# Three buffers for gathered keys, a gather one step ahead, and a denser decode, in a hybrid decoder step on one core

## The chip, the core and the metric

The kernel runs on one core of a Trainium2 chip. The metric is the time of one execution on the device in microseconds; lower is better. TensorE (PE) multiplies, VectorE (DVE) and ScalarE (ACT) work element by element, GpSimd (POOL) issues the gathers, and SyncE (SP) issues the plain loads.

## What is computed

One layer of a decoder, for a prompt of 512 tokens and for 8 decode rows that each look back on 4096 cached tokens. Each token goes through a norm, one wide projection, two mixers (softmax attention with a forget bias, "fox", and gated linear attention, "gla"), two sigmoid gates, an output projection `w_o`, and an MLP with squared ReLU. What the change touches is the attention of the 8 decode rows over their paged cache, and the reuse of the MLP's weights for these rows:

```python
def _fox_sample(q, k_new, v_new, logf_new, k_past, v_past, logf_past):
    ...
    lp = (jnp.einsum('bqhd,bkhd->bhqk', q, k_past).astype(F32) * scale
          + jnp.swapaxes(suffix, 1, 2)[:, :, None, :] + cn[..., None])
    ...
    num = (jnp.einsum('bhqk,bkhd->bqhd', pp, v_past.astype(F32))
           + jnp.einsum('bhqk,bkhd->bqhd', pn, v_new.astype(F32)))

def _finish(x, o_fox, o_gla, gfox, ggla, w_fox_out, w_gla_out, w_o, ...):
    u = (jax.nn.sigmoid(gfox) * (o_fox.astype(dt) @ w_fox_out)
         + jax.nn.sigmoid(ggla) * (o_gla.astype(dt) @ w_gla_out))
    x = x + _rmsnorm(u @ w_o, g_post_mix)
    h = _rmsnorm(x, g_pre_mlp)
    m = jnp.square(jax.nn.relu(h @ w_up)) @ w_down
    return x + _rmsnorm(m, g_post_mlp)
```

Keys and values of the cache are 64 MB each, in pages of 128 tokens that a table lists.

## The kernel before

The main line runs the prompt through its stages: projections (`fox_q`, `fox_k`, `fox_v`, `gla_qk`, `gla_vo`), the gate blocks (`gate_f`, `gate_g`, `mix`), `w_o` with its norms (`post`, `wo_each`, `wo_fin`), and four chunks of the MLP, `up(c)` and `down(c)`. Dense products run as three matmuls each on a weight that is split in a high and a low part (L221 on ScalarE, L222 on VectorE). `post` ends with a tail: the last 256 columns are computed block by block of 128 rows, and `wo_fin` then makes the norm of that block (L1182, L216, the power L217 on GpSimd, the sum L1184, eight transposes, L326 and a split).

The decode is a generator of 144 steps, `decode()`: 9 rounds of 16. Step (b, g) scores two of a row's 32 slices of keys for row b (gathered tile `kk` of 0.5 MB, multiply L573 and reduction L574 on VectorE) and, on every second step, multiplies a 1 MB tile of values (`kv`) for row b-1 on TensorE into `pdv`. The last step of a round ends a row: bias, maximum, exponentials (L603 to L619). A gather is issued by `page_load` (L208) on GpSimd's queue; `LK` and `LV` say how many steps ahead, and `BU` how many buffers a tag has. The main line calls `pump(rate)` at every yield: it adds the matmul columns issued since the last call (in units of 2400) times `rate / TAU` to a debt and advances the decode one step per whole unit of debt:

```python
        owed[0] += (clock[0] - seen[0]) * rate / TAU
        while owed[0] >= 1 and (scored[0] or count[0] < NG):
            owed[0] -= 1
```

`PA` to `PE_`, `PF` and `PG` are the rates of the stages. The gate blocks and mixes run at `PC`, the main part of `w_o` at `PD`, its tail at `PF`, the first yields of the MLP at `PG`, the rest at `PE_`. The scheduler below this code places instructions of each engine in an order of its own, in which program order is the priority; every engine then works through its own list in that order.

When the decode is over, `sample_mix` (queued as a side task, one step per yield) takes the 8 rows through gates, `w_fox_out`, `w_o` and the norms and sets `mixed`. From then on `up` carries the 8 rows as extra columns of its own matmuls (`dense_fm2`). Weights that went by earlier are listed in `late` and loaded a second time by `sample_mlp` (tag `kv`, two loads of 0.5 MB for each weight, `sproj_ps` from the unsplit weight). `down(c)` uses its own tile for the 8 rows only where `whole[c]` says that no `up` weight of the chunk was late.

Of the kernel before, what the change touches and what calls it, by code (L numbers as in the profile page):

```python
# [19 lines left out]
NB = 8  # L20
# [3 lines left out]
EPS = 1e-6  # L24
TS = T + NB
FP, LP, LQ = 3, 1, 1
PA, PB, PC, PD, PE_ = 1, 1.2, 0.6, 0.6, 1
LK, LV = 0, 2
TO = 1
PF, PG, HN = 0.8, 1.5, 2  # L30
BU = dict(h=4, c8=9, wh=6, wl=5, raw=5, kk=2, kv=2, td=2, ts=5, qb=2, tj=1, ev=1)
PK = 2
TAU = 3.1
MS = 1
# [1 line left out]
NG, NV = 32 // KJ, 32 // VJ  # L36
# [13 lines left out]
def _emit(ctx, tc, I, O):  # L50
# [591 lines left out]
    def pump(rate):  # L642

        owed[0] += (clock[0] - seen[0]) * rate / TAU
        while owed[0] >= 1 and (scored[0] or count[0] < NG):
            owed[0] -= 1
            count[0] += 1
            if next(dec, "end") == "end":
                over[0] = True
        seen[0] = clock[0]  # L650
# [393 lines left out]
    side = []  # L1044
# [226 lines left out]
            V.tensor_tensor(out=d, in0=p[:, 0:256], in1=d, op=ALU.add)  # L1271
        first[n] = False

    late, whole, mixed = [], [True] * 4, [False]

    def sample_mlp():

# [9 lines left out]
    def up(c, ah, al):  # L1287
# [7 lines left out]
        for n in range(4):  # L1295
            w = take()[0]
            with_sample = mixed[0] and not (c == 0 and n < HN)
            if not with_sample:
                whole[c] = False
                late.append((wup, c, n))  # L1300
            if c == 0 and n < HN:
                for r in (slice(0, 256), slice(256, 512)):
# [19 lines left out]
    def down(c):  # L1322
        def take_(n):
            w, _, raws = take()
            if not whole[c]:
                late.append((wdn, c, n))
            else:
                sample_acc(n, sproj_ps(aS[:, c * 8:c * 8 + 8, :], raws, "x"))
            if c == 3 and n == 3:
                sample_end()  # L1330
            return w
# [25 lines left out]
    def sample_end():  # L1357
        while not over[0]:
            owed[0] += 1
            pump(0)  # L1360
        start_mix()
        drain("mix", "mlp")
        y, x = new_["y"], new_["x"]
        for n in range(2):
            p = ps("x")
            mm(p[0:8, :], sel[:, 0:8], new_["acc"][n], True, True)
            S.copy(out=y[n][0:8, :], in_=p[0:8, :])
        sample_post(y, "g_post_mlp", x)
        for i in range(2):
            nc.sync.dma_start(out=O["y_sample"].rearrange("b l d -> (b l) d")[:, i * 512:(i + 1) * 512], in_=x[i][0:8, :])  # L1370

    def dense_mlp(gen, n, first=()):
        for i, _ in enumerate(gen):
            pump(first[i] if i < len(first) else n)
            if over[0]:
                start_mix()
            beside(MS)

    started = [False]

    def start_mix():
        if not started[0]:
# [40 lines left out]
```

## Time and profile before

| what | value |
|---|---|
| median of three runs | 1068.72 us (1062.19 to 1077.32) |
| the profiled execution | 1074.91 us, span 1073.2 us |
| busy: PE, DVE, ACT, POOL | 93%, 64%, 40%, 25% of the span |
| mean granted clock of TensorE | 0.964 |
| gathers | 128 of keys, 64 of values, 8 of log-forgets |

A busy share is an average over stages; the rows below give it by stage. An instruction's line is that of the helper that records it (L84 for all matmuls), so the tile names tell which product it is: `pmm` the dense products, `pdv` the decode's values, `px` the small products beside.

The stages in the profiled execution, by the first instruction of each on ScalarE or VectorE: projections to 283 us, `gate_f` to 408, `gate_g` and `mix` to 521, `w_o` to 608 (its main part ends about 565), `up(0)` and `down(0)` to 721, and the other three chunks to the end.

### The profile page before, as it was taken

To read this page: it belongs to the slowest core of one execution; us is meant where nothing else is said; L and a number is where in the kernel's file an instruction comes from. 1 tells how busy PE (TensorE), PEld (TensorE's weight loads), DVE (VectorE), ACT (ScalarE), POOL (GpSimd) and SP (SyncE) were. 2 spreads that over 40 slices of the span, in tenths; PEclk is the share of its full clock that TensorE was granted. 3 is DMA by queue.
4 is the path that set the end of the run, shared out by engine and by line. 5 is a ranking of instruction groups with operands and counts; after the bars stand their busy time and mean duration, and the time that the engine had idled before them with its cause. 6 is when DMAs were issued, how large, how long until landed. Compare 5 with 4: busy or idle time off the path is not lost.

```text
span 1073.2 us, 20743 instructions
## 1 busy us (share of the span) xinstructions
PE 995.3 (93%) x8183; PEld 828.5 (77%) x8183; DVE 689.9 (64%) x1238; ACT 426.8 (40%) x1110; POOL 272.8 (25%) x256
## 2 busy tenths in 40 slices
PE   6988899999999899999894799999999799999996
PEld 5987777877967788787683677787787588888995
DVE  8568766876988858887769769667233333233356
ACT  6424444444743423333233443325423453115442
POOL 5132333244332324423434332430100000000001
PEclk9998999999999979999997899999999899999998
DMA  6736788688478637966995687894667366677222
GB/s 199 240 129 209 228 298 289 207 298 309 141 280 311 190 114 254 324 200 209 340 335 178 218 306 260 318 348 138 217 228 239 123 205 213 211 236 233 82 75 86
DMA packets 134279, 242.03 MB, mean 226 GB/s; under 512 B 11627, under 2 KB 105150, under 8 KB 125990
## 3 DMA queue, kind: packets, MB, share of 16 engines
q0 software_dynamic: 28032, 135.28, 35.7%
q1 hardware_dynamic: 106150, 105.43, 31.0%
q8 instruction: 64, 1.05, 0.4%
q14 instruction: 33, 0.27, 0.1%
HBM read 235.14 MB, written 5.47 MB: 224 GB/s over the span
## 4 chain that ended last, share of the span: by engine, by line
PE 64%; DMA 19%; issue 7%; DVE 6%; POOL 1%; ACT 1%; SPq 0%; DVEq 0%; POOLq 0%; ACTq 0%
PE pmm L84 47%; DMA kk<-in_cache_k,ixki 12%; PE px L84 10%; PE pdv L84 5%; DMA kv<-in_cache_v,ixvi 2%; DVE kk L573 2%; DMA kv<-in_w_up 1%; DVE sc L574 1%; DMA kv<-in_w_down 1%; PE pd L84 1%; DMA c<-in_state_gla 1%; DVE wl L222 1%; PE px L684 1%; POOL kk L208 0%; ACT tj L344 0%
## 5 line engine op out<-in xcount | busy, mean ns | idle before, releaser
L84 PE MATMUL pmm<-h,wh 128*128 128x256 f32 (+2 forms) x1696 | 358.7, 307 | 9.9 <-ACT h L221 4.1
L84 PEld LDWEIGHTS pmm<-h,wh 128*128 128x128 f32 x1696 | 276.7, 193 | 47.0 <-issue 19.5
L84 PE MATMUL pmm<-h,wl 128*128 128x256 f32 (+2 forms) x848 | 257.3, 306 | 0.8 <-DVE wl L222 0.8
L208 POOL DMA_INDIRECT kk<-in_cache_k,ixki x128 | 166.2, 1298 | 342.1 <-DVE sc L574 214.2
L84 PE MATMUL pmm<-wh,c 128*128 128x256 f32 x1280 | 233.1, 283 | 6.4 <-DVE c L1039 4.5
L84 PEld LDWEIGHTS pmm<-wh,c 128*128 128x128 f32 x1280 | 196.7, 189 | 28.2 <-issue 16.7
L573 DVE TENSOR_TENSOR kk<-kk,qb 128x1024 f32<-128x1024 f32 x128 | 156.5, 1223 | 92.6 <-DMA kk<-in_cache_k,ixki 90.3
L222 DVE TENSOR_TENSOR wl<-raw,wh 128x512 fp32r<-128x512 f32 x240 | 162.0, 687 | 79.4 <-PE pmm L84 55.8
L221 ACT CAST wh<-raw 128x512 fp32r<-128x512 f32 x240 | 146.4, 619 | 160.9 <-PE pmm L84 99.0
L84 PE MATMUL pmm<-wl,c 128*128 128x256 f32 x640 | 178.8, 282 | 1.6 <-DVE wl L222 1.6
L84 PEld LDWEIGHTS pmm<-h,wl 128*128 128x128 f32 x848 | 162.8, 193 | 12.6 <-issue 4.6
L574 DVE TENSOR_REDUCE sc<-kk 128x16 f32<-128x1024 f32 x128 | 154.9, 1212 | 0.7
L84 PEld LDWEIGHTS pmm<-wl,c 128*128 128x128 f32 x640 | 120.6, 189 | 10.4 <-issue 7.9
L208 POOL DMA_INDIRECT kv<-in_cache_v,ixvi x64 | 69.5, 1086 | 141.1 <-PE pdv L84 115.6
L217 POOL TENSOR_TENSOR rs<-rs,mhalf 128x1 f32<-128x1 f32 (+2 forms) x21 | 16.3, 778 | 292.7 <-DVE rs L216 291.1
L84 PE MATMUL pmm<-wh,h 128*128 128x256 f32 x384 | 77.0, 291 | 0.0
L84 PE MATMUL pdv<-kv,pt 128*32 128x512 f32 x512 | 67.8, 610 | 5.4 <-DMA kv<-in_cache_v,ixvi 5.4
L84 PEld LDWEIGHTS pmm<-wh,h 128*128 128x128 f32 x384 | 60.9, 191 | 5.0 <-issue 4.9
L84 PE MATMUL pmm<-wl,h 128*128 128x256 f32 x192 | 56.5, 295 | 1.0 <-DVE wl L222 1.0
L1338 DVE TENSOR_TENSOR c<-pmm,c 128x256 f32<-128x256 f32 x48 | 18.7, 421 | 57.1 <-PE pmm L84 56.7
L1292 DVE TENSOR_TENSOR c<-td,c 128x256 fp32r<-128x256 f32 (+1 forms) x50 | 24.8, 497 | 32.5 <-ACT td L1291 32.2
L84 PE MATMUL pmm<-c,wh 128*128 128x512 f32 x128 | 42.6, 416 | 1.6 <-DVE c L910 1.3
(335 smaller groups left out, 1099.5 us busy)
## 6 DMA issues: line engine op xcount, KB each, us to landing
raw<-in_w_in SPq DMA_DIRECT2D x80, 256.0 KB
raw<-in_w_up SPq DMA_DIRECT2D x64, 256.0 KB
raw<-in_w_down SPq DMA_DIRECT2D x64, 256.0 KB
kv<-in_w_down SPq DMA_DIRECT2D x24, 512.0 KB
kv<-in_w_up SPq DMA_DIRECT2D x18, 512.0 KB
raw<-in_w_o SPq DMA_DIRECT2D x16, 256.0 KB
kv<-in_w_o SPq DMA_DIRECT2D x8, 512.0 KB
c<-in_x_prompt SPq DMA_DIRECT2D x4, 512.0 KB
```

Source lines behind the costliest of these rows:

```text
L84: PE.matmul(out=out, lhsT=lhsT, rhs=rhs, start=start, stop=stop)
L208: G.indirect_dma_start(out=t, out_offset=None, in_=view, in_offset=bass.IndirectOffsetOnAxis(ap=ix[:, b, g:g + 1], axis=0))
L217: G.tensor_tensor(out=r, in0=a, in1=mhalf[:P, :n], op=ALU.pow)
L221: S.copy(out=hi, in_=raw)
L222: V.tensor_tensor(out=lo, in0=raw, in1=hi.bitcast(F32), op=ALU.subtract)
L573: V.tensor_tensor(out=K3, in0=K3, in1=qb[:, None, :].to_broadcast([128, KJ, 512]), op=ALU.mult)
L574: V.tensor_reduce(out=sc[:, g * 8 * KJ:(g + 1) * 8 * KJ], in_=K.rearrange("p (x d) -> p x d", d=64), axis=AX.X, op=ALU.add)
L684: PE.transpose(out=sp[:, kb * 128:(kb + 1) * 128], in_=P[:, kb * 128:(kb + 1) * 128], identity=ident)
L1292: V.tensor_tensor(out=l, in0=r[:, 0:n], in1=d.bitcast(F32), op=ALU.subtract)
L1338: V.tensor_tensor(out=d, in0=p, in1=d, op=ALU.add)
```

## The change

The rates `PC` and `PD` go from 0.6 to 0.9. Keys have three buffers (`kk=3`), and their gather is issued one step ahead (`LK=1`); `LV` stays 2. For the last round, which has only values, a step costs half a unit of debt. The flags `whole` are gone: `down` uses its own tile for the 8 rows where no `up` weight of its chunk is still in `late`, and `catch_up` queues `sample_mlp` again whenever something is late and no side task is left.

```diff
-PA, PB, PC, PD, PE_ = 1, 1.2, 0.6, 0.6, 1
-LK, LV = 0, 2
+PA, PB, PC, PD, PE_ = 1, 1.2, 0.9, 0.9, 1
+LK, LV = 1, 2
...
-BU = dict(h=4, c8=9, wh=6, wl=5, raw=5, kk=2, kv=2, td=2, ts=5, qb=2, tj=1, ev=1)
+BU = dict(h=4, c8=9, wh=6, wl=5, raw=5, kk=3, kv=2, td=2, ts=5, qb=2, tj=1, ev=1)
...
-        while owed[0] >= 1 and (scored[0] or count[0] < NG):
-            owed[0] -= 1
+        while owed[0] >= (1 if count[0] < NB * NG else 0.5) and (scored[0] or count[0] < NG):
+
+            owed[0] -= 1 if count[0] < NB * NG else 0.5
...
-    late, whole, mixed = [], [True] * 4, [False]
+    late, mixed = [], [False]
...
             if not with_sample:
-                whole[c] = False
                 late.append((wup, c, n))
...
-            if not whole[c]:
+            if not mixed[0] or any(v is wup and e == c for v, e, _ in late):
                 late.append((wdn, c, n))
...
         start_mix()
-        drain("mix", "mlp")
+        drain("mix")
+        catch_up()
+        drain("mlp")
...
                 start_mix()
+            catch_up()
             beside(MS)
 
     started = [False]
+
+    def catch_up():
+        if mixed[0] and late and not side:
+            side.append(("mlp", sample_mlp()))
```

## Rows read from the trace of the kernel before

**Rows 1.** Busy time by stage: PE, weight loads, DVE, ACT, POOL, clock, DMA share, GB/s.

```profile
core 0: us, PE busy (x) PEld busy (x) DVE busy (x) ACT busy (x) POOL busy (x), PEclk, DMA share, GB/s
29.00:135.00 106.00, 94.55 (x746) 86.24 (x745) 73.25 (x126) 41.79 (x114) 29.48 (x22) 0.95 0.63 201
135.00:283.00 148.00, 147.30 (x1120) 113.68 (x1119) 108.85 (x166) 68.81 (x198) 56.73 (x50) 1.00 0.76 269
283.00:408.00 125.00, 117.89 (x1476) 99.25 (x1475) 103.72 (x204) 50.05 (x132) 40.42 (x32) 0.92 0.62 209
408.00:521.00 113.00, 105.70 (x746) 86.57 (x745) 91.87 (x156) 41.56 (x130) 42.77 (x35) 0.97 0.77 266
521.00:571.00 50.00, 49.35 (x401) 43.36 (x401) 34.06 (x54) 17.07 (x47) 17.34 (x17) 0.97 0.87 303
571.00:608.00 37.00, 16.32 (x99) 12.64 (x103) 34.76 (x58) 12.81 (x36) 17.65 (x14) 0.75 0.57 177
608.00:735.00 127.00, 123.76 (x836) 101.28 (x829) 91.09 (x117) 49.72 (x114) 42.68 (x39) 0.98 0.84 297
735.00:1073.00 338.00, 319.85 (x2634) 269.91 (x2632) 128.48 (x284) 126.46 (x308) 10.02 (x13) 0.98 0.54 175
```

**Rows 2.** Waits of PE over the span: us in total, times, longest.

```profile
PE px L323 <- DVE c L1184: 7.0, 1, 7.0
...
PE pdv L84 <- DMA kv<-in_cache_v,ixvi: 5.4, 3, 4.5
...
PE pmm L84 <- DVE c L1039: 4.5, 2, 4.3
...
PE pdv L609 <- DVE mx L606: 3.5, 1, 3.5
PE px L684 <- ACT ts L697: 3.3, 1, 3.3
```

**Rows 3.** The key multiplies (L573) alone by stage: us, DVE busy and their number.

```profile
29.00:283.00 254.00, 61.09 (x50) 0.98 0.71 241
283.00:408.00 125.00, 22.00 (x19) 0.92 0.62 209
408.00:521.00 113.00, 24.43 (x20) 0.97 0.77 266
521.00:571.00 50.00, 8.53 (x7) 0.97 0.87 303
571.00:608.00 37.00, 9.78 (x8) 0.75 0.57 177
608.00:735.00 127.00, 30.64 (x25) 0.98 0.84 297
```

**Rows 4.** L573: min/median/max ns, first and last start; then what DVE waited for.

```profile
L573 DVE TENSOR_TENSOR kk<-kk,qb x128: 1201/1224/1300, 39.5 to 733.7; 128x1024 f32<-128x1024 f32 x128
...
  DMA kk<-in_cache_k,ixki: 90.3, 55
```

**Rows 5.** DVE in order of time: the residual sum of two blocks of the tail.

```profile
565.34 1.28 DVE L1184 SCALAR_TENSOR_TENSOR c<-c,rs,c 128x1024 f32<-128x1024 f32 x1 [0.76 <-POOL rs L217]
...
576.40 1.28 DVE L1184 SCALAR_TENSOR_TENSOR c<-c,rs,c 128x1024 f32<-128x1024 f32 x1
```

**Rows 6.** PE in order of time: half of a second load's product, and its wait.

```profile
902.76 0.64 PE L84 MATMUL px<-kv,c 128*32 128x256 f32 x8 [0.39 <-DMA kv<-in_w_down]
```

**Rows 7.** ACT in order of time: ends of `up` blocks, undivided (740, 745) and halved.

```profile
740.02 0.59 ACT L1289 ACTIVATE td<-pmm 128x512 f32<-128x512 f32 x1
745.41 0.60 ACT L1289 ACTIVATE td<-pmm 128x512 f32<-128x512 f32 x1 [3.47 <-PE pmm L84]
...
1000.97 0.38 ACT L1289 ACTIVATE td<-pmm 128x256 f32<-128x256 f32 x1
...
1012.09 0.38 ACT L1289 ACTIVATE td<-pmm 128x256 f32<-128x256 f32 x1 [0.23 <-PE pmm L84]
```

**Rows 8.** GpSimd's gathers of keys, and busy time in a stretch with a full DVE.

```profile
L208 POOL DMA_INDIRECT kk<-in_cache_k,ixki x128: 932/1020/4222, 24.1 to 728.9; - x128
...
493.00:498.00 5.00, 5.00 (x29) 3.86 (x29) 4.71 (x8) 1.22 (x4) 4.40 (x2) 1.00 0.53 141
```

## The prediction

> **What bounds the kernel now.** I read the busy time of every engine by stage first, because the share over the whole span hides where an engine waits. TensorE (PE) is the bound: from 135 to 283 us it works 147.3 of 148 us, and from 735 to the end 319.9 of 338 [rows 1]. So a step of the decode is worth something only where PE stands still. That is in three places: 29 to 135 us (11.4 us idle), 283 to 521 us (7.1 and 7.3 us), and above all 571 to 608 us, where PE works 16.3 of 37 us while VectorE (DVE) works 34.8 of 37 and the granted clock is 0.75 [rows 1]. That last stretch is the tail of the w_o stage, four row blocks that each need a norm before the first `up` matmuls can start.
>
> Second I read what PE waited for. The longest wait is 7.0 us for DVE's L1184 (the residual sum of the tail); 3.5 us go to DVE's L606, the batch end of the decode, 4.5 us to L1039 in the mix stage, 3.3 us to a softmax row that stood behind the decode on DVE, and 5.4 us to gathers of values [rows 2]. DMA is never the name in front of PE for keys. But it is in front of DVE: DVE stood 90.3 us in 55 waits for a gather of keys [rows 4], and everything queued behind that multiply waited too.
>
> Third I counted decode multiplies by stage. Up to 283 us 50 were done, then 19, 20, 7, 8 and 25 (steps cut by a boundary count twice) [rows 3]. The loops of `pump` ask for 63 by the start of the gate blocks (283 us). So the decode ran 13 steps late there, made this up during the slow middle stages, and was level when the tail began: 95 done at 571 us, 97 asked for. The rate 0.6 was thus not the pace of the middle stages; draining the debt was. With a gather issued only at its own step and two buffers, a step in the early part took 254/50 = 5.1 us [rows 3], although two DVE passes of 1.22 us are all its work [rows 4].
>
> **The change, part by part.**
>
> *Order asked for.* A gate block yields after 24 x 520 = 12480 columns, 5.2 units of 2400: at 0.6 that is 5.2 x 0.6/3.1 = 1.0 step, at 0.9 1.5. Added up over the loops, the steps asked for at the ends of gate_f, the mixes and the main part of w_o, and at the start of `up`, go from 78, 91, 97, 100 to 86, 105, 114, 117. The scores end (128) in the fifth yield of the first `up` chunk, where they ended in the eighth of the first `down` chunk. The last batch's value steps cost half, so its eight 1 MB tiles take 33 units of 2400 columns instead of 63. `sample_mix` then starts one chunk earlier (second yield of `down(0)`, not `down(1)`), and by my count of the loops weights loaded a second time fall from 21 (9 up, 12 down) to 10 (5 and 5).
>
> *Third buffer, gather one step ahead.* Gather i+1 now needs the buffer of step i-2, as gather i did, so a key tile has a whole step more to land. On GpSimd's queue the gather that waits for its buffer stands in front of value gathers, the gather of log-forgets and the power of the norms (L217); since the wait ends with the same step as before, I add nothing there. If a gather's cycle is now shared by three buffers, the pace of 5.1 us becomes some 5.1 x 2/3 = 3.4 us (an estimate from the row), and 3.8 us are asked for up to 283 us: the decode keeps up with the order.
>
> So the steps done per stage become about 63 (50), 23 (18), 19 (19), 9 (7), 3 to 4 (8), 11 (25), at 2 x 1.22 = 2.44 us of DVE each [rows 3, 4]. The terms, against the profiled execution (1074.9 us, span 1073.2):
>
> (a) 29 to 135 us: the keys' waits go; of 11.4 us idle only 3.3 us are plainly behind them. Bounds 0 and -7; I take **-4**.
> (b) To 283 us, 13 steps more are 32 us on DVE, 182 + 32 = 214 of 254 us. PE has no idle to lose, only DVE lateness to suffer: 0 to +6, taken **+2**.
> (c) 283 to 408 us: 5 steps more, 103.7 + 12 = 116 of 125 us on DVE (93%). Bounds 0 and +12 (all on the path); **+4**, since PE still ran 117.9 of 125 at 83% [rows 1].
> (d) 408 to 521 us: the same number of steps, without the waits for keys that delayed L1036 and L1039: 0 to -5, **-4**.
> (e) 521 to 571 us: two steps more, 2 MB in 50 us, 303 + 40 = 343 GB/s, where 303 at a share of 0.87 puts the full pipe at 348 (estimate): 0 to +4, **+1**.
> (f) The tail. Now the blocks are 11.1 us apart (L1184 at 565.34 and 576.40 [rows 5]), as eight decode steps (8 x 2.44 = 19.5 us of DVE's 34.8) and a batch end stand between. After it three or four steps are left, and the batch end (step 111) falls before the tail; DVE's need drops to about 22 us. PE's idle time falls from 20.7 us to some 5, and the lost clock (0.75) comes back for about 3 us: **-19**, bounds -5 (the debt is carried into the tail) and -24.
> (g) The last batch's tiles at twice the pace: 8 MB in about 36 us beside weights. The nearest row is PE's 5.4 us for values in three waits, longest 4.5 [rows 2]; 0 to +8, **+3**.
> (h) Late: a reload is two groups of eight matmuls of 0.64 us and up to 0.39 us of wait [rows 6], 1.7 us. Four fewer of w_up: -6.7; seven of w_down become a product from the loaded tile at the same PE cost, less a wait now and then, -1. Against that eight more blocks run as 48 matmuls of 256 and 264 columns instead of 24 of 512: 5.56 us a block (1000.97 to 1012.09, two blocks) against 5.39 (740.02 to 745.41) [rows 7], +1.4. Sum **-6**, bounds -8 and 0. The direct products hold their raw tiles until PE comes; `down(3)` does so already.
>
> Everything else (end of the decode, sample norms, last `down`) moves and costs the same. Sum: -4 +2 +4 -4 +1 -19 +3 -6 = -23, so 1051.9 for an execution like the profiled one. The median of the runs is 6.2 us below that execution, so I put 1068.7 - 23 = **1046** us.
>
> One row speaks against the pace: a gather of keys occupies GpSimd 1.02 us in the median but up to 4.22, and in 493 to 498 us, with DVE busy 4.71 of 5 us, two instructions took GpSimd 4.40 us [rows 8]. A denser DVE could so slow the gathers it feeds on. If all took 4.2 us, three buffers would still give about (5.1 x 2 + 3.2)/3 = 4.5 us a step: enough for the middle (5.5 us asked), not for the early part (3.8). The Trainium skill, page "SBUF — State Buffer", section "Who interferes with whom", says that a VectorE instruction with two SBUF inputs, as the multiply of L573 has, contends with a GpSimd instruction that reads SBUF, and that the second to come blocks fully. By that rule the forecast turns into the second rival below; the row agrees in sign, while the median of 1.02 us says that it is rare so far.
>
> **The rivals.**
> 1. *The order is not kept* (the change does not do what it says): gathers are held by GpSimd or by a DMA at 0.77 to 0.87 of its time from 408 to 571 us [rows 1], the decode still carries a debt, and eight steps stand in the tail again. Then (f) is -5, (a) and (d) -1 each, (b) and (c) 0: -1 -1 +1 -5 +3 -6 = -9, 1060 us. For it: the late pace was 127/25 = 5.1 us too, where DVE had room [rows 1, 3].
> 2. *DVE becomes the bound* (slower). It works in order, and once it has more than about 94% to do, PE starves as in the tail (34.8 of 37 us against PE's 16.3). If that point is reached from 135 to 571 us, the 20 added steps lie on the path: 49 us in place of the 7 of (b), (c), (e), and (a) and (d) give nothing: -23 + 42 + 8 = +27, 1096 us. Against it: my sums are 84, 93, 81 and 78%, and only (c) comes near.
> 3. *All of it comes*: waits at their far bounds, -7 -5 -24 -8 = -44, 1025 us, and no cost.
>
> **How the numbers follow.** Forecast 0.42 (its own range 1035 to 1058), the order not kept 0.30, DVE the bound 0.10, all of it 0.18. The range that leaves out 2 in 10 runs from 1024 to 1074. A measurement of this kernel tells 2% from no change, 1047.3 us here: half of the forecast's own range and all of rival 3 lie below, 0.22 + 0.18 = 0.40; rival 1 and the rest within, 0.50; rival 2 above, 0.10.
>
> **What would show it.** Right: about 63 multiplies done by the gate blocks, three or four between the last w_o matmul and the first `up`, PE's idle there below 8 us, the waits for keys (90.3 us) more than halved, 10 and 10 second loads of w_up and w_down (each weight is two loads) instead of 18 and 24. Wrong: DVE over 94% with new PE waits for L222, L1035 or L1173; a tail with eight steps again; or long PE waits for gathered values in the first `down` chunk.

## The result and the profile after

The changed kernel takes 1086.66 us in the median of six runs, against 1070.75 us for the kernel before in six runs on the same chip: a ratio of 1.0155, with a 95% interval of 1.0114 to 1.0196. The forecast was 1046 us, with a range of 1024 to 1074. It is slower by about 16 us where 23 us were to be gained; the interval lies wholly above 1 and below 1.02. The profiled execution took 1086.9 us, span 1085.2 us, at a mean granted clock of 0.948 (before 0.964).

Busy time by stage, for the stretches of [rows 1]:

```profile
core 0: us, PE busy (x) PEld busy (x) DVE busy (x) ACT busy (x) POOL busy (x), PEclk, DMA share, GB/s
29.00:135.00 106.00, 82.76 (x622) 74.53 (x622) 84.15 (x122) 32.38 (x84) 40.14 (x29) 0.84 0.67 210
135.00:283.00 148.00, 146.09 (x1122) 113.41 (x1121) 117.92 (x181) 65.49 (x202) 62.74 (x57) 1.00 0.83 298
283.00:408.00 125.00, 117.13 (x1336) 90.76 (x1335) 109.94 (x200) 57.24 (x157) 53.00 (x40) 0.93 0.76 259
408.00:521.00 113.00, 101.06 (x826) 80.83 (x825) 98.25 (x170) 35.74 (x107) 48.83 (x44) 0.88 0.81 281
...
571.00:608.00 37.00, 34.67 (x277) 31.32 (x276) 24.84 (x39) 11.07 (x33) 10.69 (x11) 0.95 0.87 305
608.00:735.00 127.00, 117.67 (x856) 93.92 (x855) 55.36 (x111) 56.80 (x140) 17.66 (x18) 0.97 0.58 196
```

The loss is in the first line: 82.8 us of TensorE work in 106 us where [rows 1] have 94.6, at a clock of 0.84 for 0.95. The stretches further down no longer hold the same work, since everything after it starts late: `gate_f` begins about 36 us later, `w_o` about 44 us later. The key multiplies by stage, as in [rows 3] (from here on lines from L646 to L1298 have numbers one higher than before):

```profile
29.00:283.00 254.00, 75.31 (x62) 0.93 0.76 261
283.00:408.00 125.00, 29.26 (x24) 0.93 0.76 259
408.00:521.00 113.00, 27.97 (x23) 0.88 0.81 281
521.00:571.00 50.00, 12.08 (x10) 1.00 0.85 301
571.00:608.00 37.00, 8.14 (x7) 0.95 0.87 305
608.00:735.00 127.00, 2.75 (x3) 0.97 0.58 196
```

62 multiplies are done by 283 us, where [rows 3] have 50 and I had asked for 63; 126 are done by 608 us, where before had 104 of them. By the clock the decode thus ran ahead as forecast. By the stages it ran further ahead than that, since they stand later: 69 multiplies had begun when `gate_f` did (about 320 us) and 119 when `w_o` did (about 565 us), where 63 and 105 were asked for. DVE's wait for keys (duration min/median/max in ns; then us, times) fell from 90.3 us in 55 waits [rows 4] to 36.0 in 30:

```profile
L573 DVE TENSOR_TENSOR kk<-kk,qb x128: 1200/1218/1277, 39.7 to 612.6; 128x1024 f32<-128x1024 f32 x128
...
  DMA kk<-in_cache_k,ixki: 36.0, 30
```

The tail of w_o stands at 609 to 634 us now, with no key multiplies left in it after 612.6 us; its residual sums (L1185 here) are as far apart at the start as in [rows 5], 11.6 us, because two key steps and the last batch end (L603 at 619.5 us) stand between them; the next two follow 7.5 and 5.6 us later:

```profile
609.61 1.27 DVE L1185 SCALAR_TENSOR_TENSOR c<-c,rs,c 128x1024 f32<-128x1024 f32 x1
...
621.21 1.26 DVE L1185 SCALAR_TENSOR_TENSOR c<-c,rs,c 128x1024 f32<-128x1024 f32 x1
...
628.70 1.28 DVE L1185 SCALAR_TENSOR_TENSOR c<-c,rs,c 128x1024 f32<-128x1024 f32 x1 [0.45 <-POOL rs L217]
...
634.26 1.28 DVE L1185 SCALAR_TENSOR_TENSOR c<-c,rs,c 128x1024 f32<-128x1024 f32 x1
```

What TensorE waited for, as in [rows 2]:

```profile
PE pdv L84 <- DMA kv<-in_cache_v,ixvi: 20.9, 9, 7.0
PE pd L338 <- DVE qb L335: 10.2, 1, 10.2
PE pmm L84 <- DVE wl L222: 9.8, 4, 2.9
...
PE px L908 <- DVE ts L904: 4.2, 2, 2.8
...
PE pdv L84 <- ACT pt L619: 2.8, 1, 2.8
...
PE pd L418 <- DVE lft L378: 2.5, 1, 2.5
```

Waits for values are up from 5.4 us in three to 20.9 in nine. The tail's 7.0 us (L1184), the 4.5 us for L1039 and the 3.3 us for the softmax row of [rows 2] are no longer among the waits of 1.9 us or more. Waits for weight splits (L222) are up from 3.3 us to 9.8, three of the four (8.3 us) between 79 and 97 us; the one for the log forgets (L378) is up from 1.5 to 2.5, and the one for the norm of the samples (L335) from 6.3 to 10.2.

To place the loss I use one measure throughout: **TensorE's lost time** in a window of 25 us is 25 minus its busy time multiplied by the granted clock of the window, so idle time and lost clock count together. It is approximate, since the clock is the mean of the window, and it is taken from one execution of each kernel. Summed over stretches, in us:

| kernel | 0-75 | 75-125 | 125-275 | 275-425 | 425-525 | 525-650 | 650-725 | 725-850 | 850-1050 | sum |
|---|---|---|---|---|---|---|---|---|---|---|
| before | 11.6 | 12.7 | 0.7 | 18.9 | 10.7 | 28.8 | 2.5 | 6.7 | 5.1 | 97.7 |
| changed | 11.4 | 30.5 | 1.9 | 14.8 | 23.5 | 17.0 | 0.8 | 19.7 | 0.0 | 119.6 |
| e1 buffer and gather ahead alone | 11.6 | 30.7 | 4.9 | 15.1 | 28.9 | 21.9 | 0.0 | 0.0 | 12.6 | 125.7 |
| e2 rates alone | 10.6 | 10.2 | 3.0 | 18.1 | 10.2 | 31.9 | 2.6 | 44.5 | 7.5 | 138.6 |
| e3 half steps, catch_up alone | 10.0 | 7.8 | 3.0 | 20.9 | 11.0 | 30.5 | 1.4 | 23.5 | 0.2 | 108.3 |
| e4 changed, old buffers | 10.9 | 7.9 | 1.9 | 19.4 | 8.4 | 30.0 | 4.1 | 71.1 | 0.0 | 153.7 |
| e9 changed, third buffer held | 10.7 | 11.1 | 0.0 | 15.5 | 23.7 | 21.1 | 0.0 | 12.1 | 0.0 | 94.2 |
| e10 rate 0.9 in w_o alone | 10.1 | 10.1 | 1.4 | 18.3 | 11.5 | 30.3 | 1.9 | 18.3 | 0.1 | 102.0 |
| e12 changed, old rates | 10.0 | 31.1 | 1.1 | 13.6 | 29.4 | 20.1 | 0.0 | 3.7 | 1.0 | 110.0 |
| e13 as e9, not in gla_out | 11.2 | 10.9 | 0.0 | 13.0 | 12.5 | 36.8 | 3.7 | 18.9 | 0.0 | 107.0 |

The tail's gain is there (28.8 to 17.0), and so is a little in the gate stage. Against it stand 18 us at 75 to 125 us, 13 at 425 to 525, and 13 at 725 to 850 (5 of which before had after 850 us). The lost time rises by 22 us, the span by 12; the rest I put to weights loaded a second time (42 loads before, 20 now), which was not measured by itself.

How far one execution can be trusted shows where two kernels have the same lists of instructions over a stretch. The changed kernel and e5 (below) agree within 5 us in every column. But e13 and e14, which are the same up to the last batch's values, lose 13.0 and 28.8 us at 275 to 425 us. The early column (75 to 125 us) is steadier: 29.3 to 31.1 us in the five kernels with three buffers from the start, and 7.8 to 12.7 in the ten in which as many key steps as before stand ahead of the log forgets.

**Where the early loss sits.** VectorE in order of time in the kernel before (start, duration, engine, line). L377 is the chain of small dependent operations that makes the log forgets, L378 ends it, L573 and L574 are the two passes of a key step:

```profile
77.73 0.25 DVE L377 SCALAR_TENSOR_TENSOR lf<-lf,lf 128x32 f32<-128x32 f32 x2
77.91 1.20 DVE L574 TENSOR_REDUCE sc<-kk 128x16 f32<-128x1024 f32 x1
79.04 0.17 DVE L377 SCALAR_TENSOR_TENSOR lf<-lf,lf 128x32 f32<-128x32 f32 x1
79.14 0.15 DVE L378 SCALAR_TENSOR_TENSOR lfs<-lf,lf 8x8 f32<-8x8 f32 x1
79.24 0.65 DVE L377 SCALAR_TENSOR_TENSOR lf<-lf,lf 128x32 f32<-128x32 f32 x3
79.81 1.22 DVE L573 TENSOR_TENSOR kk<-kk,qb 128x1024 f32<-128x1024 f32 x1
80.94 0.19 DVE L378 SCALAR_TENSOR_TENSOR lft<-lf,lf 128x32 f32<-128x32 f32 x1
```

And in the changed kernel:

```profile
83.13 0.24 DVE L377 SCALAR_TENSOR_TENSOR lf<-lf,lf 8x8 f32<-8x8 f32 x2
83.42 1.23 DVE L573 TENSOR_TENSOR kk<-kk,qb 128x1024 f32<-128x1024 f32 x1
84.56 0.25 DVE L377 SCALAR_TENSOR_TENSOR lf<-lf,lf 8x8 f32<-8x8 f32 x2
86.70 1.23 DVE L573 TENSOR_TENSOR kk<-kk,qb 128x1024 f32<-128x1024 f32 x1 [1.89 <-DMA kk<-in_cache_k,ixki]
87.84 1.21 DVE L574 TENSOR_REDUCE sc<-kk 128x16 f32<-128x1024 f32 x1
88.97 0.24 DVE L377 SCALAR_TENSOR_TENSOR lf<-lf,lf 8x8 f32<-8x8 f32 x2
...
100.33 0.18 DVE L378 SCALAR_TENSOR_TENSOR lft<-lf,lf 128x32 f32<-128x32 f32 x1
```

Before, the last links run up to three at a time and the log forgets of the prompt are made at 80.94 us, behind 10 key multiplies. After, one or two key passes of 1.2 us stand behind every one or two links, and the log forgets are made at 100.33 us, behind 18. The eight steps more, at 2.43 us by the medians of the two passes, are 19.4 us, and that is the delay (100.33 - 80.94). Everything behind them on VectorE, the splits of the next weights among it, comes as late, and TensorE runs dry. The two kernels over the same stretches, before first:

```profile
75.00:125.00 50.00, 41.63 (x319) 35.26 (x317) 36.84 (x63) 19.04 (x54) 13.65 (x11) 0.90 0.65 197
400.00:500.00 100.00, 98.53 (x746) 82.67 (x743) 82.47 (x147) 34.89 (x107) 38.08 (x32) 0.97 0.74 248
```

```profile
75.00:125.00 50.00, 29.07 (x182) 23.66 (x181) 42.51 (x66) 10.87 (x29) 19.73 (x15) 0.66 0.63 196
400.00:500.00 100.00, 87.53 (x854) 69.08 (x853) 85.54 (x157) 33.50 (x104) 45.24 (x42) 0.89 0.85 298
```

In 75 to 125 us TensorE does 29.07 us of work instead of 41.63, and the granted clock, which stands at 2.4 GHz (1.00) in the full stretches, is 0.66 in the mean here, between that and the lower level of 1.2 GHz (0.5), while TensorE stands idle for 20.9 us of the 50.

### The profile page after: what moved, and what is told of

Its sections match the earlier page's. It is cut to its first block, busy times and chain, and to the rows that moved or that the text cites. A ratio compares the mean times of both kernels' runs of the same rounds, so it can differ in the third digit from the quotient of the medians.

```text
span 1085.2 us, 20996 instructions
## 1 busy us (share of the span) xinstructions
PE 994.4 (92%) x8295; PEld 834.9 (77%) x8295; DVE 689.3 (64%) x1250; ACT 429.0 (40%) x1134; POOL 282.1 (26%) x256
## 4 chain that ended last, share of the span: by engine, by line
PE 61%; DMA 16%; DVE 10%; issue 8%; POOL 3%; ACT 1%; SPq 0%; POOLq 0%; DVEq 0%; ACTq 0%
PE pmm L84 46%; PE px L84 8%; DMA kv<-in_cache_v,ixvi 6%; PE pdv L84 5%; DMA kk<-in_cache_k,ixki 5%; DVE sc L574 2%; POOL kk L208 2%; DVE kk L573 2%; DMA raw<-in_w_o 2%; DVE wl L222 1%; PE pd L84 1%; DMA kv<-in_w_o 1%; PE px L685 1%; DMA kv<-in_w_down 1%; DMA c<-in_x_prompt 1%
## 5 line engine op out<-in xcount | busy, mean ns | idle before, releaser
L84 PE MATMUL pmm<-h,wh 128*128 128x256 f32 (+2 forms) x1824 | 363.1, 297 | 7.4 <-ACT wh L221 3.5
L84 PEld LDWEIGHTS pmm<-h,wh 128*128 128x128 f32 x1824 | 292.3, 193 | 34.7 <-issue 17.3
L84 PE MATMUL pmm<-h,wl 128*128 128x256 f32 (+2 forms) x912 | 268.4, 297 | 8.3 <-DVE wl L222 8.3
L222 DVE TENSOR_TENSOR wl<-raw,wh 128x512 fp32r<-128x512 f32 x240 | 162.2, 686 | 122.9 <-PE pmm L84 99.0
L208 POOL DMA_INDIRECT kk<-in_cache_k,ixki x128 | 167.8, 1311 | 233.8 <-DVE sc L574 138.4
L84 PEld LDWEIGHTS pmm<-h,wl 128*128 128x128 f32 x912 | 174.9, 193 | 20.5 <-DVE wl L222 9.1
L573 DVE TENSOR_TENSOR kk<-kk,qb 128x1024 f32<-128x1024 f32 x128 | 155.5, 1218 | 38.3 <-DMA kk<-in_cache_k,ixki 36.0
L574 DVE TENSOR_REDUCE sc<-kk 128x16 f32<-128x1024 f32 x128 | 154.1, 1209 | 1.2 <-ACT pt L619 0.7
L208 POOL DMA_INDIRECT kv<-in_cache_v,ixvi x64 | 75.6, 1181 | 161.7 <-PE pdv L84 150.8
L84 PE MATMUL pdv<-kv,pt 128*32 128x512 f32 x512 | 77.6, 645 | 23.7 <-DMA kv<-in_cache_v,ixvi 20.9
L1290 ACT ACTIVATE td<-pmm 128x256 f32<-128x256 f32 (+1 forms) x58 | 23.5, 405 | 70.6 <-PE pmm L84 67.0
```

The source lines that it names most:

```text
L84: PE.matmul(out=out, lhsT=lhsT, rhs=rhs, start=start, stop=stop)
L208: G.indirect_dma_start(out=t, out_offset=None, in_=view, in_offset=bass.IndirectOffsetOnAxis(ap=ix[:, b, g:g + 1], axis=0))
L222: V.tensor_tensor(out=lo, in0=raw, in1=hi.bitcast(F32), op=ALU.subtract)
L573: V.tensor_tensor(out=K3, in0=K3, in1=qb[:, None, :].to_broadcast([128, KJ, 512]), op=ALU.mult)
L574: V.tensor_reduce(out=sc[:, g * 8 * KJ:(g + 1) * 8 * KJ], in_=K.rearrange("p (x d) -> p x d", d=64), axis=AX.X, op=ALU.add)
L1290: S.activation(out=r[:, 0:n], in_=p[:, 0:n], func=AF.Relu)
```

## The experiments

The kernel is built with `schedule_with_timeline_sim=True`: the order of each engine's instructions is settled at building, by a simulated time, and need not be the order in which the kernel's source gives them. So the built lists can be compared without a chip. Three counts from them are used below: the key multiplies ahead of the prompt's log forgets on VectorE (before 10, changed 18; for the samples' own, just ahead, 9 and 16); those ahead of the tail's first residual sum (94 and 126); and the projection matmuls between the first and the last value product of the last batch on TensorE (185 and 191).

My first theory was that the gather ahead causes the early loss and that the denser rates do little. The rival: the rates do the harm. The first four kernels take the change apart.

**e1.** Before with `LK = 1`, `kk=3`.

> Before, with the third buffer and the gather one step ahead alone (LK 1, kk 3; rates, half steps and catch_up as before). Theory (ready keys fill every gap of VectorE's list while the chain of the log forgets is emitted, so the weight splits of that stage come late): the loss of 62 to 118 us is here too, the fox_k and fox_v projections start some 20 us later than before, TensorE works about 22 of 43 us in 75 to 118 us; the decode is ahead by 283 us (about 63 multiplies), the tail of w_o is shorter by 5 to 10 us, total about +8 us: 1.00 to 1.015 of before. Rival (the denser rates do the harm, through VectorE or the value gathers): no late stage at 75 to 118 us and total 0.975 to 0.995.

Measured: 1102.3 us, 1.0293 (1.0232 to 1.0355). The early loss is there to the microsecond (30.7), so the rival falls for that stretch; the size was missed (1.0 to 1.015 was expected), because the loss at 425 to 525 us is here too (28.9) without any change of rates.

**e2.** Before with

```
-PA, PB, PC, PD, PE_ = 1, 1.2, 0.6, 0.6, 1
+PA, PB, PC, PD, PE_ = 1, 1.2, 0.9, 0.9, 1
```

> Before, with the rates 0.9 in the gate, mix and w_o stages alone (two buffers, gather at its own step, no half steps, no catch_up). Theory (the early loss comes from the gather ahead, the middle loss from denser steps): the first 283 us are those of before within 3 us; from 283 to 571 us the debt is drained anyway, so at most 5 us are lost; total 0.99 to 1.005. Rival (the rates do the harm): +15 us or more, 1.01 to 1.02, lost from 283 us on.

Measured: 1113.7 us, 1.0395 (1.0343 to 1.0446). The first 283 us are those of before, as the theory said. But no theory of mine had the rest: next to nothing is lost or gained up to 725 us in sum (86.6 us against 85.9), the multiplies done by 283, 408, 521 and 571 us are 50, 70, 88 and 96 (before 50, 69, 88, 95), and then 44.5 us are lost at 725 to 850. TensorE in order of time there:

```profile
732.45 0.39 PE L84 MATMUL pmm<-h,wl 128*128 128x512 f32 x1
737.19 0.38 PE L609 MATMUL pdv<-ident,mx 128*8 128x128 f32 x1 [4.35 <-DVE mx L606]
...
742.11 3.64 PE L84 MATMUL pdv<-kv,pt 128*32 128x512 f32 x16 [3.33 <-ACT pt L619]
...
749.93 1.93 PE L84 MATMUL pdv<-kv,pt 128*32 128x512 f32 x8 [4.18 <-DMA kv<-in_cache_v,ixvi]
753.25 1.94 PE L84 MATMUL pdv<-kv,pt 128*32 128x512 f32 x8 [1.38 <-DMA kv<-in_cache_v,ixvi]
...
784.69 1.20 PE L84 MATMUL pmm<-h,wh 128*128 128x512 f32 x2
```

Between 732.45 and 784.69 us there is no projection matmul at all. The last batch's values stand as one block, each tile behind the first two waiting for its gather into one of two buffers; behind them come the decode's end and the mix, and the weights of `up` wait for ScalarE, whose next casts stand behind the copies that end the batch (ScalarE's next cast of a weight after 727.1 us is at 787.2). In the built list the number of projection matmuls between these values is 0, where before has 185.

**e3.** Before with the half step in `pump` and `catch_up` alone (rates 0.6, two buffers, `LK = 0`).

> Before, with the half steps of the last batch's values and catch_up alone. Theory: the mix starts one chunk earlier, 6 to 11 weight blocks fewer are loaded a second time, nothing changes ahead of the first down chunk: total 0.985 to 0.997 (some 5 to 15 us gained). Rival (the 1 MB tiles at twice the pace stand in front of TensorE): 1.00 to 1.01, with waits for values of over 10 us in the first down chunk.

Measured: 1081.53 us, 1.0095 (1.0064 to 1.0127). The rival was right: in the list 22 projection matmuls are left between the last values, 10.9 us are waited for them in five waits, and 23.5 us are lost at 725 to 850 us.

**e4.** The changed kernel with `LK = 0`, `kk=2`.

> The changed kernel with two buffers and the gather at its own step again (rates, half steps and catch_up stay). Theory (the gather ahead makes the early loss): TensorE works 33 or more of 43 us in 75 to 118 us again, fox_k and fox_v start within 4 us of before, the whole is 15 to 30 us shorter than the changed kernel: 0.985 to 1.00 of before. Rival (the rates do the harm): within 6 us of the changed kernel, 1.01 to 1.02 of before.

Measured: 1121.07 us, 1.0458 (1.0407 to 1.0509). The early loss is gone (7.9), as the theory had it, but the block (no projection matmul between the values, 71.1 us lost) outweighs it. Neither theory had the total. Each part alone costs, and the buffer takes back a part of what the others cost: with it the scores all but end before the tail, and the values are again spread.

So the theory was formed anew: a key step takes its place on VectorE's list as soon as a buffer is free for its gather. The number of buffers sets the decode's pace, and through that what stands ahead of the other chains; the rates only say where in TensorE's list the values stand, and asking faster than the decode runs puts them en bloc.

**e5.** The changed kernel with `LK = 0` (three buffers stay).

> The changed kernel with its three buffers and the gather at its own step again (LK 0). Theory now (each engine's list of instructions is settled when the program is built, and a key step takes its place as soon as a buffer is free for its gather; so the number of buffers counts and the step at which the gather is written does not): the lists of all five engines are, instruction by instruction, those of the changed kernel, and so is the time: 1.0115 to 1.0196 of before. Rival (the gather ahead stands on GpSimd's list in front of values and norms and costs by itself): 8 us or more away from the changed kernel.

Measured: 1087.15 us, 1.0189 (1.0112 to 1.0267). The lists of all five engines are the same, instruction by instruction, with the gather ahead and without it: the "gather one step ahead" changes nothing in this kernel.

**e6.** Before with a third buffer for the first batch's keys alone:

```
-BU = dict(..., kk=2, kv=2, ...)
+BU = dict(..., kk=2, kx=1, kv=2, ...)
-                pk.append(page_load(kvw, ixki, nk // NG, nk % NG, KJ, "kk"))
+                pk.append(page_load(kvw, ixki, nk // NG, nk % NG, KJ, "kx" if nk < NG and nk % 3 == 2 else "kk"))
```

> Before, with the third buffer for the keys of the first batch alone. Its VectorE list has 17 key multiplies ahead of the result of the log-forget chain, where before has 9 and the changed kernel 16. Theory (the places in VectorE's list make the early loss): TensorE's lost time (idle, and busy time times one minus the granted clock) from 75 to 125 us is 28 to 33 us as in the changed kernel (30.5), before 12.7; afterwards the decode is about a batch end's work ahead and the tail of w_o gives back 5 to 10 us; total 1.005 to 1.015 of before. Rival (the early loss comes from the gather ahead or from the denser rates): 10 to 15 us lost there, total 0.99 to 1.003.

Measured: 1109.01 us, 1.0371 (1.0299 to 1.0443). 24.3 us are lost at 75 to 125 us, and 9.0 already at 25 to 50 us, where before loses 0.9. The early loss needs neither the gather ahead nor the rates. The tail gave nothing back (30.1), though I had expected it to; the time is a miss by 2%.

**e7.** The changed kernel, `LK = 0`, `kk=2, kx=1`, `"kx" if nk >= 4 * NG and nk % 3 == 2 else "kk"`.

> The changed kernel with the third buffer used from the keys of the fifth batch on only (tile 64 and later) and LK 0. Its VectorE list has 11 key multiplies ahead of the log forgets (before 9, changed 16), 108 ahead of the first residual sum of the w_o tail (94, 125), and 194 projection matmuls between the last batch's values (185, 191). Theory (places in the lists): 12 to 17 us lost at 75 to 125 us, under 8 us in the w_o tail (before 17), no block of values; total 0.975 to 0.995 of before. Rival (three gathers in flight slow GpSimd, VectorE and the other transfers wherever they are used): from 300 to 600 us it loses as the changed kernel does and more, and ends at 1.005 or above.

Measured: 1094.31 us, 1.0259 (1.0186 to 1.0332). At 75 to 125 us it loses 13.0, as the theory said, with 13 key multiplies ahead of the prompt's log forgets, which are made at 90.53 us. So ten of the changed kernel's 19 us of delay cost next to nothing there: the loss does not grow in step with the delay. The total is a miss: 33.2 us are lost at 725 to 850, 18.2 at 425 to 525, 26.9 at 525 to 650. The total follows the rival; the place doesn't (it expected the loss from 300 to 600 us).

**e8.** The changed kernel without the half step (`while owed[0] >= 1 ...: owed[0] -= 1`).

> The changed kernel with whole steps for the last batch's values (catch_up, rates and three buffers stay). Its TensorE list has 273 projection matmuls between the last batch's first and last values (changed 191). Theory: the block of values in the first up chunk is looser, the waits for values of 600 to 700 us (9.3 us) fall to 4 or less, but 6 more weight blocks are loaded a second time (about 10 us): total within 6 us of the changed kernel, 1.01 to 1.02 of before. Rival (the half step is what costs): 10 us or more shorter than the changed kernel, 1.005 or below.

Measured: 1083.43 us, 1.0144 (1.0078 to 1.021): the changed kernel's time. The half step is worth nothing that can be measured here, at 16 and 16 second loads instead of 10 and 10. The waits for values at 600 to 700 us fell to 7.0 us, not to 4. The loss at 725 to 850 us is gone (0.9).

**e9.** The changed kernel, `LK = 0`, `kk=2, kx=1`, with its third buffer withheld by a dummy until the prompt's log forgets are done:

```
+        hold[0] = new([128, KJ * 512], "kx")          # in decode(), first lines
+        V.memset(hold[0][:, 0:32], 0.0)
...
+        V.tensor_tensor(out=hold[0][:, 0:32], in0=hold[0][:, 0:32], in1=lft.rearrange("p t h -> p (t h)"), op=ALU.add)
...
-                pk.append(page_load(kvw, ixki, nk // NG, nk % NG, KJ, "kk"))
+                pk.append(page_load(kvw, ixki, nk // NG, nk % NG, KJ, "kx" if nk >= 16 and nk % 3 == 2 else "kk"))
```

The dummy only keeps the buffer taken; the sum that is added to it is used by nothing.

> The changed kernel with its third key buffer held by a small dummy until the log forgets of the prompt are done, and used from tile 16 on for every third tile (one addition of 128 by 32 on VectorE and one small fill more). VectorE's list has 9 key multiplies ahead of the log forgets, as before (changed 16); 61 projection matmuls stand between the values of the seventh batch (changed 216). Theory (the early loss is the key steps ahead of the log-forget chain): TensorE's lost time at 75 to 125 us falls from 30.5 to 12 to 16 us, fox_k starts within 4 us of before; total 10 to 20 us below the changed kernel, 0.995 to 1.006 of before, less up to 10 us if the seventh batch's values become a block. Rival (the early loss comes from something else that three gathers bring, GpSimd or DMA): 25 us or more lost there still.

Measured: 1062.77 us, 0.992 (0.9892 to 0.9948), 24 us below the changed kernel and the only one of all that beats the kernel before, by 0.8% (its interval lies below 1, and within 2% of it). The log forgets, and then the stretches of the two fences above:

```profile
79.67 0.18 DVE L378 SCALAR_TENSOR_TENSOR lft<-lf,lf 128x32 f32<-128x32 f32 x1
```

```profile
75.00:125.00 50.00, 44.08 (x331) 38.21 (x330) 42.69 (x69) 20.89 (x58) 17.41 (x14) 0.86 0.70 220
400.00:500.00 100.00, 83.21 (x610) 65.44 (x608) 89.62 (x154) 26.97 (x90) 52.50 (x39) 0.86 0.82 281
```

They are made at 79.67 us, behind 10 key multiplies as before. In 75 to 125 us TensorE works 44.08 us at 0.86, and 11.1 us are lost instead of 30.5. That is 19.4 us of the 24; the others are 7.6 us less at 725 to 850 us, 4 more in the tail, and what the measure doesn't catch. The decode runs hardly slower than in the changed kernel (59 multiplies by 283 us and 118 by 571 us, against 62 and 119). So in the early stretch it is not the decode's pace that costs, but where eight of its steps stood. The third buffer is in use in e9 too by 88.6 us, when its first tile is multiplied, at a DMA share of 0.70 and without that loss. The loss at 400 to 500 us stays.

**e10.** Before with `PD = 0.9` alone (`PA, PB, PC, PD, PE_ = 1, 1.2, 0.6, 0.9, 1`).

> Before with rate 0.9 in the w_o stage alone (0.6 in the gate and mix stages, two buffers, whole steps, no catch_up). Its VectorE list has 94, 97, 99, 101 key multiplies ahead of the four residual sums of the w_o tail, exactly as before and as the kernel with 0.9 in all three stages, and 188 projection matmuls stand between the last batch's values (before 185; with 0.9 everywhere none). Theory (the rates don't set the decode's pace; they only say where the last values stand, and 0.9 everywhere puts them en bloc): no loss at 725 to 825 us, total 0.995 to 1.01, some 35 us below the kernel with 0.9 in all three stages (1.0395). Rival (denser steps cost by themselves): 1.015 to 1.035, in between.

Measured: 1071.51 us, 1.0024 (0.9996 to 1.0052): the time of before, 42 us below e2, from which it differs by `PC` alone. In the list 188 projection matmuls stand between the last values again. The block is thus the cost of the rates, and no other shows; the 18.3 us in the table lie behind 825 us, at a wait of 9.0 us for the norm of the samples.

**e11.** As e9 with `nk >= 48` and without the half step.

> As the kernel with the held third buffer, but used from the fourth batch's keys on (tile 48), and with whole steps for the last values. Lists: 9 key multiplies ahead of the log forgets, 103 to 276 projection matmuls between the values of every batch (no block), 234 for the last. Theory: early loss as before, the w_o tail's loss under 8 us (before 16.6 and 8.0), no block at the end: total 0.98 to 0.995 of before, the first to beat it. Rival (the middle stages lose with three buffers whatever the early order: 425 to 500 us): over 20 us lost there, total 1.00 to 1.01.

Measured: 1089.29 us, 1.0168 (1.0118 to 1.0218). A miss, and the rival's loss is there: 27.8 us at 425 to 525 us; 31.0 more at 525 to 650 us, where three waits of 4.2 to 4.5 us for batch ends, norms and casts stand. No block at the end, and no gain from that.

**e12.** The changed kernel with rates 0.6.

> The changed kernel with rates 0.6 in the gate, mix and w_o stages again (three buffers, half steps, catch_up). Its VectorE list has the same 16, 18 and 81 key multiplies ahead of the chains and 123 to 128 ahead of the w_o tail (changed 125 to 128); 122 projection matmuls stand between the last batch's values (changed 191). Theory (the rates do not set the pace): up to 600 us TensorE's lost time is that of the changed kernel within 6 us; what differs lies after, in the block of the last values; total 1.012 to 1.03. Rival (the denser rates are what loses in the middle): 10 us less lost by 500 us, total 1.005 or below.

Measured: 1089.65 us, 1.0206 (1.0152 to 1.026). Multiplies done by 283, 408, 521 and 571 us are 62, 87, 110 and 117, with 0.9 they are 62, 86, 109 and 119. With three buffers too the rates set no pace, and the total is within the theory's range.

With that the early loss and the block were settled. Open was the loss at 400 to 500 us: key passes inside gla_out's chain, or the traffic of the gathered values.

**e13.** As e9 with `"kx" if (16 <= nk < 64 or nk >= 104) and nk % 3 == 2 else "kk"`.

> As the kernel with the held third buffer (0.992), with that buffer not used for tiles 64 to 103, so that gla_out runs beside two buffers. VectorE's list has 6 key passes in all between the scaling of the square sums and the four products of gla_out (held 15, before 3, changed 5); 113 to 119 key multiplies ahead of the w_o tail. Theory (the middle loss is key passes inside gla_out's chain and batch ends on VectorE, and values that come more often): TensorE's lost time at 400 to 500 us falls from 28.3 to 10 to 18 us (before 4.8), the tail stays under 12 us; total 0.978 to 0.992 of before. Rival (the middle loss is only the traffic of the gathered values): at most 5 us less lost there, total 0.990 to 1.00.

Measured: 1082.02 us, 1.0083 (1.0043 to 1.0123). The windows (400 to 500 us, and the tail):

```profile
400.00:500.00 100.00, 96.81 (x721) 78.07 (x723) 84.92 (x145) 34.74 (x106) 40.08 (x37) 0.97 0.83 285
575.00:625.00 50.00, 27.91 (x173) 21.76 (x173) 45.17 (x76) 19.18 (x50) 21.88 (x18) 0.69 0.56 193
```

With two buffers beside gla_out the loss at 400 to 500 us falls from 28.4 us (100 - 83.21 x 0.86 in e9) to 6.1 (100 - 96.81 x 0.97), and the waits for its products (L907 in e9, L903 before) from 7.7 us to 1.0, those for values from 4.7 to 1.5. That is the theory's number, but both kinds of wait fell together, so the runs don't part them. And the time came back elsewhere: a batch end now lies in the tail of w_o, which works 27.91 of 50 us at 0.69. The total is a miss. The fall itself stands in a second execution of the same lists: at 425 to 525 us e13 loses 12.5 us and e14, which is next, 9.7, where e9 and e15 lose 23.7 and 25.3.

**e14** and **e15.** As e13 and as e9, without the half step.

> As the one before, with whole steps for the last batch's values: 242 projection matmuls between them instead of 194. Theory: the loss at 750 to 800 us for the norm of the samples goes (it did so in the changed kernel with whole steps), 6 weight blocks more are loaded a second time: within 8 us of the one before, either way. Rival (half steps are what gains): 10 us or more slower.

> The kernel with the held third buffer from tile 16 on, with whole steps for the last values (273 projection matmuls between them, 61 between the seventh batch's). Theory: the early gain stays, the loss of 12 us at 750 us goes, reloads cost about 10 us more: 0.985 to 0.998 of before. Rival (the kernel with the held buffer gained through the half steps): 1.000 or above.

Measured: 1085.4 us, 1.0102 (1.0064 to 1.014), and 1067.6 us, 0.9981 (0.9939 to 1.0023). In both the loss at 725 to 850 us is small (4.6 and 1.0, against 18.9 and 12.1), as expected, and in neither does it shorten the kernel by more than can be measured. e15 differs from e9 by 0.6%, and its interval reaches from the theory's range past the rival's 1.000, so this run doesn't part them, and a gain over the kernel before isn't shown with whole steps. But e15 is 16 us below e8, the same kernel without the dummy: the buffer withheld gains with half steps and without.

## Why the prediction was wrong

**Order asked for.** This step fell first. I worked out how many steps `pump` asks for and took a faster rate for a faster decode. e2, e10 and e12 show that the rates 0.6 and 0.9 give the same count of steps at every stage, with two buffers and with three. My numbers by stage (63, 23, 19, 9) came out as 62, 24, 23, 10, but the third buffer made them, and the agreement is in part luck: these are stretches of time in which the stages no longer stand. By stages the decode was 6 to 14 steps further than was asked.

**Third buffer, gather one step ahead.** Right in effect, 36 us of waits instead of 90, and wrong in that the gather ahead has a part in it: the lists are the same without it (e5).

**(a) and (b), -4 and +2.** The step that failed. "PE has no idle to lose, only DVE lateness to suffer" priced the 13 added steps as a sum of VectorE's time (182 + 32 of 254 us, and the stretch did end with VectorE at 79 and 80% busy), not by what they would stand in front of. Eight more of them stand ahead of the end of the log-forget chain (seven ahead of the samples' part of it): 8 x 2.43 = 19.4 us, by which the log forgets came later, and 18 us were lost at 75 to 125 us; that the two numbers lie so close isn't shown to be more than chance (e7). Instead of 2 us gained by (a) and (b) together it is 18 lost. e9 takes those steps away from the chain, nearly leaves the decode's pace, and wins back 19 us there.

**(c), (e), +4 and +1.** No cost shows: 275 to 425 us lost 14.8 us instead of 18.9, VectorE 88% busy. But the gate stage stands 36 us later, and e13 and e14 show that one execution doesn't fix this column to 4 us. (e) was not measured by itself.

**(d), -4.** Wrong in sign: 425 to 525 us lost 23.5 us instead of 10.7. The stage that runs there is partly an earlier one than before, by the delay. e1 and e12 show the loss with the old rates, e9 without the early delay (23.7), and e13 that it goes when the third buffer does; which part is gla_out's chain and which the values was not parted, so its cause stays open.

**(f), -19.** Right mechanism, size off: the stretch with the tail lost 17.0 us instead of 28.8, -12, within my bounds. No key step is left in its second half, but the last batch's end stands in the tail (L603 at 619.5 us), and the longest wait there, 7.0 us, is for a tile of values of the batch before. The prediction also read its rows too widely: its eight steps are those of 571 to 608 us, and between the two sums of [rows 5] stood three, with the batch end (L603 at 577.60 us) behind the second.

**(g), +3.** The last batch's own values were waited for 0.8 us, so the term is within its bounds in the changed kernel. What I missed is that the half step has this price only because the third buffer lets the scores end early; alone it makes a block (e3). The values of the batches before cost more: 20.9 us of waits in all against 5.4.

**(h), -6.** The loads fell to 10 and 10 as counted. That the mix and the samples' last norm come in another place brought a wait of 10.2 us for the norm. Before it was 6.3 us, the second longest wait of TensorE and not among the [rows 2] shown; the prediction had the sample norms cost the same. The transposes of its result stand in TensorE's list ahead of dense products. TensorE in order of time in the changed kernel:

```profile
780.96 1.02 PE L338 MATMUL pd<-ident,qb 8*128 8x8 f32 x8 [10.20 <-DVE qb L335]
```

It goes with the second loads. All six kernels with 10 and 10 of them have it, at 8.6 to 10.2 us (the changed one, e4, e5, e7, e9, e13); the three with 18 and 24 have it later, at 5.1 to 6.3 us (before, e1, e6); of the eight with 16 and 16 seven have none of it, and e10 has 9.0 us. So the loads that were saved and this wait came together, which is one reading of why the kernels with and without the half step lie so close (e8, e14, e15). What decides it in e10 stays open.

**The rivals.** The first, that the order is not kept, is refuted by the counts. The second had the sign and the engine, but not the place or the condition: I made it depend on VectorE having more than 94% to do, and it decided at 79%, since a chain of dependent operations doesn't need a full engine to be late. The row that spoke against the pace [rows 8] didn't decide: key gathers on GpSimd took 947 ns in the median (before 1020), though the longest was 6503 (4222). The row of the gathers (min/median/max ns):

```profile
L208 POOL DMA_INDIRECT kk<-in_cache_k,ixki x128: 935/947/6503, 21.1 to 606.6; - x128
```

The multiply of L573 took 1218 ns (1224). The Trainium skill, page "SBUF — State Buffer", section "Who interferes with whom", says that a VectorE instruction with two SBUF inputs contends with a GpSimd instruction that reads SBUF. The trace agrees on GpSimd's side, which the medians hide: of the 192 gathers of keys and values before, the 62 that began beside an idle VectorE or beside L574, which has one input, took 0.93 to 0.95 us each, and of the 79 that began beside L573 or L222, which have two, 66 took over 1.1 us, up to 4.22 (in the changed kernel 73 took 0.93 to 0.99, and 55 of 68 over 1.1). So it is not rare, as the prediction had it. The longest gather of all ends only 0.9 us after VectorE comes to L574, having run instructions with two inputs almost without a break:

```profile
521.51 6.50 POOL L208 DMA_INDIRECT kk<-in_cache_k,ixki  x1 [0.71 <-DVE sc L574]
```

```profile
526.52 0.67 DVE L1040 SCALAR_TENSOR_TENSOR c<-c,c 128x512 fp32r<-128x512 f32 x1
527.12 1.20 DVE L574 TENSOR_REDUCE sc<-kk 128x16 f32<-128x1024 f32 x1
```

It decided nothing here all the same: the key gathers took GpSimd 167.8 us in all, before 166.2.

## What to carry to other kernels

Work that was ready early went into the gaps of VectorE's list here, and a chain of small dependent operations offers a gap at every link. Before giving filler work one more buffer, look at which chains it will be ready beside, and try to withhold the buffer until they are done (here one dummy tile turned +1.6% into -0.8%). A rate asked for in the source is not a pace when the order is settled by readiness: count, in the built lists, what stands ahead of each instruction that the bounding engine waits for. And take a change of several edits apart before believing a sum: here each of three parts alone cost 1 to 4%, and together 1.6%.

## What was not expected of the hardware

Little of it is the hardware's. VectorE's waits for keys fell by 54 us while the kernel became 16 us slower, and of the kernels above the four with 87 to 89 us of such waits (e2, e3, e4, e10) lie at 1.04, 1.01, 1.05 and 1.00, and e9 with 39 at 0.99: this wait says nothing of the time here. Short waits are dear where the clock falls with them: in 75 to 125 us of the changed kernel, with 20.9 us without a matmul, the granted clock was 0.66, so that the 29.07 us of matmuls done there are worth some 19.2 us at full clock (an estimate from the two). A block of values shows it most: e2 ran 735 to 775 us at a clock of 0.52 while gathers moved 184 GB/s at a DMA share of 0.55, so that neither TensorE nor the DMA engines were full; that two buffers and the order set that pace is my reading, and no run with more buffers for values tests it. The least expected is the row of the gathers above: a gather of 0.94 us became one of up to 4.25 us where it began beside a multiply or a split, and none did where it began beside a reduction.
